# Hybrid attention trunk on one core: the softmax division moved from the score tiles to the output of the product with the values

## The chip, the cores and the metric

The kernel runs on one core of one Trainium2 chip. Its time is the device time of one execution, in microseconds (us). A core has five engines that work side by side, each through its own queue in order: TensorE (PE: matmuls and transposes, with PEld for its weight loads), VectorE (DVE), ScalarE (ACT), GpSimd (POOL) and SyncE (SP, which issues the DMAs). They wait for one another through semaphores. SBUF is the working memory of 128 partitions, PSUM the memory into which PE writes its results, used by this kernel in banks of 128x512 numbers.

## The reference

The model is a trunk of two layers over 1024 latent tokens and 256 context tokens of width 1024, with 16 heads of 64. Layer 0 is a two-dimensional neighbourhood attention with a learned bias, layer 1 a sliding window attention (128 to either side) with 4 groups of keys and values for the 16 heads and one sink logit per head. In both, each latent token reads its neighbourhood and all context tokens in one softmax; in layer 0 the context tokens attend to one another as well. Each layer ends with a gated feed-forward network with a short convolution. What the change touches is the softmax and the product behind it:

```python
def attend(q, k, v, bias=None, mask=None, sink=None):
    s = jnp.einsum('...qngd,...knd->...ngqk', q, k).astype(jnp.float32) * (HEAD_DIM ** -0.5)
    if bias is not None:
        s = s + bias.astype(jnp.float32)
    if mask is not None:
        s = jnp.where(mask, s, NEG_INF)
    if sink is not None:
        sink_col = ...
        s = jnp.concatenate([s, sink_col], axis=-1)
    p = jax.nn.softmax(s, axis=-1)
    if sink is not None:
        p = p[..., :-1]
    return jnp.einsum('...ngqk,...knd->...qngd', p.astype(v.dtype), v)
...
    for i in range(DEPTH):
        ...
        h = modulate(rmsnorm(x, g_attn[i]), sh1, sc1)
        ...
        x = x + gt1 * (o @ w_out)
        if not last:
            o_c = attend(q_c, k_c, v_c, sink=sink).reshape(bsz, n_ctx, D_MODEL)
            ctx = ctx + gt1c * (o_c @ w_out)
        h = modulate(rmsnorm(x, g_ffn[i]), sh2, sc2)
        x = x + gt2 * conv_ffn(h, ffn_w_up[i], ffn_conv_w[i], ffn_conv_b[i], ffn_w_down[i])
        ...
```

## The kernel before

**Precision.** Matmuls run on numbers of type fp32r. An operand is split into a high part (its copy in fp32r) and a low part (the difference to the original), and a product is made of two or three matmuls: names that end in hi and lo, such as whi, wlo, pthi, ptlo, are these parts. A projection of one tile of 128 tokens is 8 x 3 matmuls (mm<-whi,h0hi and its two partners).

**Stages.** The program runs the modulation and the norms, then the attention of layer 0 (about 60 to 720 us of the profile), its output projection and feed-forward network, the attention of layer 1 (about 1720 to 2190 us) and again projection and network. The change touches the two attention stages only.

**Units.** `plan_su` plans one unit of attention. A unit has two halves k = 0 and 1, each a block of 128 queries of one head. In layer 0 (`plan_na_su`) a unit is a head pair hp (of 8), a slice su (of 5: four of 256 latent queries, and one, su = 4, of the 256 context queries) and a head e of the pair; its halves are the two blocks of the slice. That makes 80 units. In layer 1 (`plan_sw_su`) a unit is a group g (of 4), a block j of 128 queries (of 8) and a pair of heads pr; its halves are the two heads. That makes 64 units. For each half:

1. PE makes the scores, in layer 0 in PSUM banks named s, in layer 1 in one wide tile with a place for each half. Queries lie on the partitions, keys along the row.
2. DVE passes over the scores (bias or mask added, sign turned, the row's extreme found) and writes them to the tile S in SBUF.
3. ACT takes the exponential in place and adds up each row: the sum goes to the small tile sm.
4. DVE takes the reciprocal of sm (one instruction per half in layer 0, one for both halves in layer 1).
5. DVE or ACT multiplies the whole of S by it, 256 to 640 columns: `TENSOR_SCALAR S<-S,sm` or `ACTIVATE S<-S,sm`.

Then, for both halves together and in two or three groups of up to two key blocks:

6. PE transposes the blocks of S (pt<-idr,S) into a PSUM bank pt, so that keys lie on the partitions.
7. ACT writes the high part (pthi<-pt), DVE the low part (ptlo<-pt,pthi).
8. PE multiplies both by the values (pv<-pthi,v and pv<-ptlo,v), all into one bank pv. Values are split too, with high and low part side by side, so that the first 64 partitions of pv hold the product with the high part and the other 64 that with the low part.
9. ACT copies one half of pv to SBUF (pvup<-pv), and DVE adds the two into the output tile osb (osb<-pv,pvup), where the outputs lie transposed: head dimension on the partitions, two heads one above the other, queries along the row.

An output tile osb covers 256 queries in layer 0 (both heads e) and 512 in layer 1 (four blocks j); when full it is stored by a DMA on SP's queue (o_dram<-osb), or, in the last head pair or group, split at once for the output projection.

**What sets the order.** `Sched` gets every operation with its candidate engines, an assumed duration, what it reads and writes, a key, and the buffers that it takes (acq) and gives back (rel). It then plays the whole stage through, on each engine always the ready operation with the lowest key, and an operation may only start if its buffers are free: for pt two PSUM banks, for pv one, for qsq, osb and the parts two SBUF buffers each. Where an operation has two candidate engines, the one that would finish it first by this reckoning gets it. The result is one fixed order per engine, in which the instructions are issued. So a change of one operation moves many others. Between the units stand, by their keys, the projections for the next head pair or group; they are most of what PE has to do besides the units, and there are fewer of them per unit in layer 1 than in layer 0.

All instructions come through a helper at line 79, so the profile's rows are told apart by their tile names.

Of the kernel before, what the change touches and what calls it, by code (L numbers as in the profile page):

```python
# [241 lines left out]
def trunk_kernel(ctx, tc, xperm, xseq, cc, wmod, bmod, gnorm, na_wqkv, na_gq, na_gk, na_bias, na_wo,  # L242
# [187 lines left out]
    def t_dve(n):  # L430
        return 0.065 + n / 960.0

    def t_act(n):
        return 0.094 + n / 1200.0
# [164 lines left out]
    def plan_su(sc, key, I, units, groups, psa, wk, reads, write, n_add, wide=None, at=None):  # L599
# [33 lines left out]
        if wide is not None:  # L633
            for k in range(2):
# [4 lines left out]
                def scores(e, k=k, nl=nl):  # L639
                    if k == 0:  # L640
                        J["sm"] = tiny.tile([P, 2, 2], F32, tag="sm", name="sm", bufs=4)
# [15 lines left out]
        for k in range(2):  # L657
# [3 lines left out]
            def ctx_part(e, k=k):  # L661
                u = J["u", k]
                if k == 0:
                    J["sm"] = tiny.tile([P, 2, 2], F32, tag="sm", name="sm", bufs=4)
# [29 lines left out]
        for k in range(2):  # L694
            n = TC + units[k]["nl"]
# [6 lines left out]
            if wide is None:  # L702
                sc.op("dve", 0.08, rec, reads=[K("P", k)], writes=[K("r", k)], key=key)
            elif k == 0:
                sc.op("dve", 0.09, rec, reads=[K("P", 0), K("P", 1)], writes=[K("r", 0), K("r", 1)], key=key)
# [446 lines left out]
    def plan_na_su(n):  # L1152
# [47 lines left out]
        ok = ("osb", hp, su)  # L1200

        def write(sc, J, K):
# [6 lines left out]
            if e == 0:  # L1209
                return  # L1210
            if hp < HP - 1:
# [11 lines left out]
        plan_su(sc, key, I, units, groups, psa, wk, reads, write, 1)  # L1223
# [1084 lines left out]
    def plan_sw_su(n):  # L2308
# [29 lines left out]
        ok = ("osb", g, j // 4, pr)  # L2338

        def write(sc, J, K):  # L2340
# [17 lines left out]
        plan_su(sc, key, I, units, [lst[i:i + 2] for i in range(0, len(lst), 2)], psa, wk, reads, write, 2, wide, at)  # L2358
# [169 lines left out]
```

## Time and profile before

| | |
|---|---|
| time, median of 3 runs (lowest to highest) | 2945.76 us (2944.11 to 2946.61) |
| span of the profiled execution, which is the time that the page gives of it | 2945.7 us |
| PE busy | 2826.0 us, 96% |
| PEld busy | 2459.7 us, 84% |
| DVE busy | 2383.5 us, 81% |
| ACT busy | 1725.9 us, 59% |
| POOL busy | 790.4 us, 27% |
| DMA | 367.51 MB, mean 125 GB/s |
| exponentials of score halves | 288 |
| transposes of score blocks | 1280 |

In the rows of the profile, `out<-in` gives the tiles, then come the shapes as partitions x elements. In the timeline a row begins with its start and its length in us, and a bracket at its end gives the idle time of its engine before it and what ended that. In the tables of groups, `x76` is a count, and behind the first bar stand the busy time in us and the mean length in ns. In the list of waits the engine that waited stands left of the arrow, its releaser right of it, then the total in us, how often, and the longest. A table of stretches gives busy us per engine, the clock that PE was granted (1.00 is full), the share of the DMA engines and GB/s. The score pass in layer 1 appears as `CUSTOM_DVE_ANT_0 S<-wide,bandt,small` followed by a read of its accumulator m; in the program's order it is written `ISA`.

### The profile page before, as it was taken

To read this page: it belongs to the slowest core of one execution; us is meant where nothing else is said; L and a number is where in the kernel's file an instruction comes from. 1 tells how busy PE (TensorE), PEld (TensorE's weight loads), DVE (VectorE), ACT (ScalarE), POOL (GpSimd) and SP (SyncE) were. 2 spreads that over 40 slices of the span, in tenths; PEclk is the share of its full clock that TensorE was granted. 3 is DMA by queue.
4 is the path that set the end of the run, shared out by engine and by line. 5 is a ranking of instruction groups with operands and counts; after the bars stand their busy time and mean duration, and the time that the engine had idled before them with its cause. 6 is when DMAs were issued, how large, how long until landed. Compare 5 with 4: busy or idle time off the path is not lost. (4 is left out here: it accounts for less than half of the span.)

```text
span 2945.7 us, 45913 instructions
## 1 busy us (share of the span) xinstructions
PE 2826.0 (96%) x16344; PEld 2459.7 (84%) x16344; DVE 2383.5 (81%) x4788; ACT 1725.9 (59%) x3389; POOL 790.4 (27%) x867
## 2 busy tenths in 40 slices
PE   6999999999999999999989999999899999999999
PEld 4999999998889977777778888988877687777787
DVE  7888888889688777877886878888877887888757
ACT  4777777778456544444544568887763544444443
POOL 2222222122100033313430135544521123433200
PEclk9999999999999999999999999999999999999999
DMA  6222222215645544444464630100144333233655
GB/s 239 62 86 79 87 62 74 86 60 153 229 162 183 178 150 147 140 150 148 154 240 163 194 119 30 33 12 14 73 127 145 102 103 100 90 100 129 242 158 186
DMA packets 138838, 367.51 MB, mean 125 GB/s; under 512 B 20848, under 2 KB 30448, under 8 KB 137200
## 3 DMA queue, kind: packets, MB, share of 16 engines
q1 hardware_dynamic: 138608, 364.57, 37.5%
q8 instruction: 129, 2.11, 0.3%
q14 instruction: 101, 0.83, 0.1%
HBM read 297.53 MB, written 66.98 MB: 124 GB/s over the span
## 5 line engine op out<-in xcount | busy, mean ns | idle before, releaser
L79 DVE TENSOR_TENSOR wlo<-wraw,whi 128x512 fp32r<-128x512 f32 (+1 forms) x245 | 298.4, 1218 | 40.4 <-ACT whi L79 38.3
L79 ACT ACTIVATE whi<-wraw 128x512 fp32r<-128x512 f32 (+1 forms) x264 | 212.3, 804 | 173.0 <-PE ud L79 45.4
L79 ACT ACTIVATE whi<-s 128x1024 fp32r<-128x1024 f32 (+1 forms) x120 | 113.2, 944 | 256.6 <-PE uc L79 222.6
L79 DVE TENSOR_TENSOR ptlo<-pt,pthi 128x512 fp32r<-128x512 f32 (+2 forms) x384 | 221.3, 595 | 51.6 <-ACT pthi L79 49.3
L79 DVE SCALAR_TENSOR_TENSOR u<-c,cv,u 128x1023 f32<-128x1023 f32 x176 | 252.2, 1448 | 8.9 <-ACT u L79 7.4
L79 PE MATMUL dn<-glo,whi 128*128 128x512 f32 x616 | 241.9, 393 | 5.8 <-DVE glo L79 5.7
L79 PE MATMUL dn<-ghi,whi 128*128 128x512 f32 x616 | 241.8, 393 | 4.2 <-ACT ghi L79 4.2
L79 ACT ACTIVATE S<-S,m 128x640 f32<-128x640 f32 (+3 forms) x288 | 220.9, 768 | 41.6 <-DVE m L79 28.6
L79 PE MATMUL dn<-ghi,wlo 128*128 128x512 f32 x616 | 241.3, 392 | 0.0
L79 ACT ACTIVATE pthi<-pt 128x512 fp32r<-128x512 f32 (+2 forms) x384 | 193.6, 524 | 72.8 <-PE pt L79 62.7
L79 PE MATMUL pt<-idr,S 128*128 128x128 f32 x1280 | 195.3, 276 | 2.6 <-DVE ptlo L79 1.0
L79 ACT ACTIVATE ghi<-graw 128x512 fp32r<-128x512 f32 x154 | 95.7, 627 | 153.7 <-PE dn L79 93.0
L79 PE MATMUL mm<-whi,h0hi 128*128 128x384 f32 x512 | 181.6, 355 | 1.6 <-ACT qraw L79 1.6
L79 POOL TENSOR_TENSOR u<-u 128x1024 f32<-128x1024 f32 x42 | 107.5, 2561 | 270.3 <-issue 105.7
L79 PE MATMUL mm<-wlo,h0hi 128*128 128x384 f32 x512 | 172.0, 336 | 0.0
L79 DVE TENSOR_TENSOR glo<-graw,ghi 128x512 fp32r<-128x512 f32 x145 | 106.0, 735 | 79.3 <-ACT ghi L79 78.8
L79 POOL TENSOR_TENSOR qy<-qv,mhalf 128x4 f32<-128x4 f32 (+2 forms) x120 | 125.6, 1047 | 164.2 <-DVE qv L79 156.7
L79 PEld LDWEIGHTS pt<-idr,S 128*128 128x128 f32 x1280 | 150.3, 142 | 12.0 <-DVE ptlo L79 1.9
L79 PE MATMUL pv<-ptlo,v 128*128 128x256 f32 (+1 forms) x688 | 151.4, 294 | 6.9 <-DVE ptlo L79 6.5
L79 DVE TENSOR_TENSOR wlo<-s,whi 128x1024 fp32r<-128x1024 f32 (+1 forms) x114 | 132.9, 1166 | 29.2 <-ACT whi L79 28.3
L79 PE MATMUL ua<-t12hi,whi 128*128 128x512 f32 x352 | 141.3, 401 | 12.3 <-ACT c L79 8.5
L79 PE MATMUL pv<-pthi,v 128*128 128x256 f32 (+1 forms) x688 | 146.6, 285 | 4.1 <-DVE osb L79 2.0
(344 smaller groups left out, 9180.3 us busy)
## 6 DMA issues: line engine op xcount, KB each, us to landing
wraw<-in_w_up_dram SPq DMA_DIRECT2D x132, 512.0 KB, 3.4
wm<-in_wmod_dram SPq DMA_DIRECT2D x80, 512.0 KB, 4.2
wraw<-in_w_down_dram SPq DMA_DIRECT2D x44, 512.0 KB, 3.6
graw<-g_dram SPq DMA_DIRECT2D x44, 512.0 KB, 4.5
wraw<-in_w_down_dram SPq DMA_DIRECT2D x88, 256.0 KB, 3.0
graw<-g_dram SPq DMA_DIRECT2D x66, 256.0 KB, 2.8
slab<-in_na_wqkv_dram SPq DMA_DIRECT2D x32, 384.0 KB, 3.2
woraw<-in_na_wo_dram SPq DMA_DIRECT2D x24, 512.0 KB, 4.8
```

The source lines that it names most:

```text
L79: r = f(*a, **k)
```

## The change

The scalings of S (step 5) and the reciprocals ahead of them (step 4) are gone: S stays undivided through transposition, split and the product with the values. A new object `Late` stands for one pair of units: in layer 0 the two heads e of a slice, in layer 1 the blocks j and j + 1 of one pair of heads. Its small tile t holds the four row sums that the exponentials of the two units write. When the second unit has its output added, `Late.plan` plans four more operations:

1. `rec`: one reciprocal of all four sums (DVE, 128x4).
2. `wide_`: a copy that spreads the four factors over 64 columns each, to a tile rb of 128x256 (ACT or DVE; rb takes one of the two buffers of qsq).
3. `tr`: two transposes of rb on PE into one of the two pt banks, which puts the factor of each query and head where the output's elements lie.
4. `mul`: DVE multiplies the output tile's 256 columns by that bank, which is then free.

Only then is the output tile stored or split. The sums are ready after the last exponential of the pair, so the first three can run before the product with the values is done; the fourth needs the added output. In all there are 40 such chains in layer 0 and 32 in layer 1, and 288 scalings and 224 reciprocals fewer. Since the order of each engine is made anew, other instructions move as well.

```diff
+    class Late:
+        def __init__(self, I, n):
+            self.I, self.n, self.t = I, n, None
+        def part(self, *a):
+            return _Half(self, *a)
+        def plan(self, sc, key, psa, wk, nsq, out, reads, writes):
+            I, n = self.I, self.n
+            toks = [I + ("sum", a, b) for a in range(n) for b in range(2)]
+            def rec(e):
+                dve.reciprocal(self.t[:, 1, :, :], self.t[:, 0, :, :])
+            sc.op("dve", 0.09, rec, reads=toks, writes=[I + ("r",)], key=key)
+            def wide_(e):
+                self.rb = wk.tile([P, nsq], F32, tag="qsq", name="rb", bufs=2)
+                copy(e, self.rb[:, :n * P].rearrange("p (a d) -> p a d", d=DH),
+                     self.t[:, 1, :, :].rearrange("p a b -> p (a b)").unsqueeze(2).to_broadcast([P, 2 * n, DH]))
+            sc.op(("act", "dve"), (t_act(n * P), t_dve(n * P)), wide_, reads=[I + ("r",)], writes=[I + ("rb",)], key=key,
+                  acq=[("qsq", I + ("rb",), 1)])
+            def tr(e):
+                self.pt = psa("pt", F32)
+                for a in range(n):
+                    pe.transpose(self.pt[:, a * P:(a + 1) * P], self.rb[:, a * P:(a + 1) * P], idf)
+            sc.op("pe", 0.107 * n, tr, reads=[I + ("rb",)], writes=[I + ("rt",)], key=key, acq=[("pt", I + ("rt",), 1)],
+                  rel=[I + ("rb",)])
+            def mul(e):
+                dve.tensor_tensor(out=out(), in0=out(), in1=self.pt[:, :n * P], op=ALU.mult)
+            sc.op("dve", t_dve(n * P), mul, reads=[I + ("rt",)] + reads, writes=writes, key=key, rel=[I + ("rt",)])
...
             def exp(e, k=k, nl=nl, ne=n + sink):
                 s = J["S", k]
                 act.activation(s[:, :ne], s[:, :ne], AF.Exp, bias=J["m", k][:, (1 if nl else 0):(2 if nl else 1)],
-                               scale=-1.0, accum_out=J["sm"][:, k, 0:1])
-            sc.op("act", t_act(n) + 0.187, exp, reads=parts, writes=[K("P", k)], key=key)
-            def rec(e, k=k):
-                if wide is None:
-                    dve.reciprocal(J["sm"][:, k, 1:2], J["sm"][:, k, 0:1])
-                else:
-                    dve.reciprocal(J["sm"][:, :, 1], J["sm"][:, :, 0])
...
-            def scale(e, k=k, n=n):
-                s = J["S", k][:, :n]
-                if e == "act":
-                    act.activation(s, s, AF.Copy, scale=J["sm"][:, k, 1:2])
-                else:
-                    ENG[e].tensor_scalar(out=s, in0=s, scalar1=J["sm"][:, k, 1:2], scalar2=None, op0=ALU.mult)
-            sc.op(("dve", "act"), (0.063 + 0.6 * n / 960.0, t_act(n)), scale, reads=[K("r", k)], writes=[K("P", k)], key=key)
+                               scale=-1.0, accum_out=norm.sum(k))
+            sc.op("act", t_act(n) + 0.187, exp, reads=parts, writes=[K("P", k), norm.tok(k)], key=key)
...
+            f["late", su].plan(sc, key, psa, wk, 256, lambda: f["o", su], [], [ok])
...
+            if j % 2:
+                lt.plan(sc, key, psa, wk, 320, lambda: f["o", pr][:, (j % 4 - 1) * P:(j % 4 + 1) * P], [], [ok])
```

More of the change, by code (lines that the diff above doesn't have):

```diff
@@ new lines, in trunk_kernel, with __init__, sum, tok @@
+    class _Half:
+        def __init__(self, late, *ab):
+            self.late, self.ab = late, ab
+        def sum(self, k):
+            L = self.late
+            if L.t is None:
+                L.t = tiny.tile([P, 2, L.n, 2], F32, tag="sm", name="sm", bufs=4)
+            a, b = [k if x is None else x for x in self.ab]
+            return L.t[:, 0, a, b:b + 1]
+        def tok(self, k):
+            a, b = [k if x is None else x for x in self.ab]
+            return self.late.I + ("sum", a, b)
@@ L600, in plan_su @@
+    def plan_su(sc, key, I, units, groups, psa, wk, reads, write, norm, wide=None, at=None):
         J = {}
@@ L1200, in plan_na_su @@
         ok = ("osb", hp, su)
+        if e == 0:
+            f["late", su] = Late(("late0", hp, su), 2)
         def write(sc, J, K):
@@ L1221, in write @@
                               key, [ok], [ok])
-        plan_su(sc, key, I, units, groups, psa, wk, reads, write, 1)
+        plan_su(sc, key, I, units, groups, psa, wk, reads, write, f["late", su].part(None, e))
     for k in range(KT):
@@ L2338, in plan_sw_su @@
         ok = ("osb", g, j // 4, pr)
+        if j % 2 == 0:
+            f["late", pr] = Late(("late1", g, j // 2, pr), 2)
+        lt = f["late", pr]
         def write(sc, J, K):
@@ L2356, in write @@
                 op1.split(j // 4, (j // 4, kt), 512, lambda: O[j // 4, pr], lambda a: a[:, kt, :], key, [ok], [ok])
-        plan_su(sc, key, I, units, [lst[i:i + 2] for i in range(0, len(lst), 2)], psa, wk, reads, write, 2, wide, at)
+        plan_su(sc, key, I, units, [lst[i:i + 2] for i in range(0, len(lst), 2)], psa, wk, reads, write, lt.part(j % 2, None), wide, at)
     for j in range(0, KT, 2):
```

11 lines of the change are left out of this document (removed).

## The prediction

> **What bounds the kernel now.** I read the page's first part, then the table of stretches, then the waits of TensorE (PE) in the two attention stretches, and last the timeline around the longest of them. The page's head says that PE is the engine to watch:
>
> ```profile
> span 2945.7 us, 45913 instructions
> PE 2826.0 (96%) x16344; PEld 2459.7 (84%) x16344; DVE 2383.5 (81%) x4788; ACT 1725.9 (59%) x3389; POOL 790.4 (27%) x867
> ```
>
> The span of this execution, 2945.7 us, is the median of the shown runs (2945.76 us) to a tenth, so I add and subtract from 2945.7. The table of stretches (length, then busy us of PE, PEld, DVE, ACT and POOL, then the granted clock) separates the two layers. Layer 0's attention lies in 60 to 690 us, layer 1's in 1720 to 2190 us:
>
> ```profile
> 60.00:690.00 630.00, 625.27 (x4481) 595.56 (x4479) 528.68 (x1881) 462.64 (x1198) 141.48 (x189) 1.00 0.26 76
> 1720.00:2190.00 470.00, 435.79 (x2949) 407.72 (x2949) 398.56 (x1070) 370.55 (x895) 227.34 (x446) 0.97 0.13 42
> ```
>
> In layer 0 PE is idle for 630 - 625.27 = 4.7 us and its clock is full: that stretch is PE's own work. In layer 1 PE is idle for 470 - 435.79 = 34.2 us, and a granted clock of 0.97 takes away up to 0.03 x 470 = 14.1 us more. So layer 1 has at most 48.3 us to give back, and layer 0 next to nothing. The waits of PE in layer 1 (us in total, times, longest) name the engine:
>
> ```profile
> PE wide L79 <- DVE m L79: 16.4, 26, 1.8
> PE pv L79 <- DVE ptlo L79: 6.2, 7, 1.7
> PE pt L79 <- DVE ptlo L79: 1.3, 3, 0.7
> ```
>
> DVE is 398.56 / 470 = 85% busy there, and PE waits for its score pass (which frees the wide score bank) and for the low half of the transposed scores. Two places show what stands ahead of such a wait. In the first it is an instruction that the change removes:
>
> ```profile
> 2150.86 2.77 POOL L79 TENSOR_TENSOR o0lo<-oraw,o0hi 128x512 fp32r<-128x512 f32 x2 [2.34 <-ACT o0hi L79]
> 2151.01 2.97 DVE L79 TENSOR_SCALAR S<-S,sm 128x640 f32<-128x640 f32 x2
> 2153.89 0.41 DVE L79 TENSOR_TENSOR ptlo<-pt,pthi 128x256 fp32r<-128x256 f32 x1
> 2154.36 0.39 PE L79 MATMUL pv<-ptlo,v 128*128 128x256 f32 x1 [1.74 <-DVE ptlo L79]
> ```
>
> Two scalings of score tiles take 2.97 us while POOL works beside them; the low half stands behind them, and PE is idle for 1.74 us. The usual length of one (min, median and max of the 76 on DVE in layer 1, ns) is 549:
>
> ```profile
> L79 DVE TENSOR_SCALAR S<-S,sm x76: 475/549/2201, 1765.5 to 2175.7; 128x640 f32<-128x640 f32 x63, 128x512 f32<-128x512 f32 x13
> ```
>
> In the second, no instruction of the change stands ahead:
>
> ```profile
> 2013.77 1.90 DVE L79 TENSOR_TENSOR v<-qraw,v 128x64 fp32r<-128x64 f32 x1
> 2015.60 0.87 DVE L79 CUSTOM_DVE_ANT_0 S<-wide,bandt,small 128x640 f32<-128x640 f32 x1
> 2017.33 0.58 PE L79 MATMUL wide<-kkc,q 128*128 128x256 f32 x1 [1.81 <-DVE m L79]
> ```
>
> **The change, part by part.** Removed are the scalings of the score tiles with their reciprocals. For the whole span, and then for the two stretches (DVE, ACT, clock):
>
> ```profile
> 0.00:2945.70 2945.70, 152.62 (x440) 54.33 (x72) 0.98 0.38 125
> 60.00:690.00 630.00, 87.60 (x279) 11.29 (x17) 1.00 0.26 76
> 1720.00:2190.00 470.00, 57.70 (x140) 40.56 (x52) 0.97 0.13 42
> ```
>
> Added are 72 chains: 8 head pairs x 5 slices = 40 in layer 0, and 4 groups x 4 pairs of blocks x 2 = 32 in layer 1. Each has one reciprocal (DVE), one copy of 128x256 that spreads the factors (by the program's order 21 on DVE and 19 on ACT in layer 0, 15 and 17 in layer 1), two PE transposes, and one DVE multiplication of 128x256 that reads PSUM. Their prices come from these rows, the PE rows being start and length:
>
> ```profile
> 304.45 0.38 PE L79 MATMUL pt<-idr,S 128*128 128x128 f32 x2
> 304.59 0.42 PE L79 MATMUL mm<-whi,h0hi 128*128 128x384 f32 x1
> 304.85 0.33 PE L79 MATMUL mm<-whi,h0lo 128*128 128x384 f32 x1
> 305.01 0.34 PE L79 MATMUL mm<-wlo,h0hi 128*128 128x384 f32 x1
> ```
>
> and for the other engines (busy us and mean ns of one behind the first bar):
>
> ```profile
> L79 DVE RECIPROCAL sm<-sm 128x2 f32<-128x2 f32 x64 | 10.1, 158 | 3.8 <-ACT S L79 3.4
> L79 DVE TENSOR_TENSOR modsb<-modsb,pt 128x256 f32<-128x256 f32 x28 | 11.7, 418 | 0.4
> L79 DVE TENSOR_SCALAR S<-S,sm 128x256 f32<-128x256 f32 x25 | 8.7, 351 | 0.4
> L79 ACT ACTIVATE st<-qn 128x256 fp32r<-128x256 f32 x80 | 33.1, 413 | 19.8 <-DVE qn L79 18.4 <-DVE sm L79 0.5
> ```
>
> PE: from the start of a pair of such transposes to the start of the second matmul behind it is 304.85 - 304.45 = 0.40 us; a matmul of 384 columns alone takes 0.17 from start to start, so a pair costs 0.23 us. That is 40 x 0.23 = 9.2 us in layer 0 and 32 x 0.23 = 7.4 us in layer 1, together 16.6 us on the busiest engine.
>
> Layer 0: PE's work is continuous, so the 9.2 us go on the path. Its 4.7 us of idle time could hide a part, which makes the ends 4.5 and 9.2; I take 9.2, since the pairs are put between matmuls that were waiting for nothing. The fences below show PE in layer 0, fourth head pair, slice 3, second head: pt<-idr,S is the transposition of scores, pt<-idr,rb that of the factors, mm is the projection for the next head pair. Before:
>
> ```order
> L79 MATMUL pv<-ptlo,v 128x256 x2
> L79 MATMUL pv<-pthi,v 128x256 x2
> L79 MATMUL pv<-ptlo,v 128x256 x2
> L79 MATMUL pt<-idr,S 128x128
> L79 MATMUL mm<-whi,h0hi 128x384
> L79 MATMUL mm<-whi,n1lo 128x384
> L79 MATMUL mm<-wlo,h0hi 128x384
> L79 MATMUL pt<-wm,cpad 32x256 x4
> L79 MATMUL pv<-pthi,v 128x128
> ```
>
> PE at the same slice in the changed program:
>
> ```order
> L79 MATMUL pv<-ptlo,v 128x256 x2
> L79 MATMUL pv<-pthi,v 128x256 x2
> L79 MATMUL pv<-ptlo,v 128x256 x2
> L79 MATMUL pt<-idr,S 128x128
> L79 MATMUL mm<-whi,h0hi_119 128x384
> L79 MATMUL mm<-whi,h0lo_123 128x384
> L79 MATMUL mm<-wlo,h0hi_119 128x384
> L79 MATMUL pt<-idr,rb 128x128 x2
> L79 MATMUL pv<-pthi,v 128x128
> ```
>
> The pair has come in ahead of the last product with the values, behind matmuls that need nothing of it; nothing idle was there to take it. The relief of DVE and ACT in layer 0 I cost at nothing, since PE hides them; without that cover they would be worth little more than the 4.7 us.
>
> Layer 1: DVE loses 57.7 us and gains 32 x 0.158 + 32 x 0.418 + 15 copies at 0.35 to 0.42 (351 and 418 ns as bounds, the middle taken) = 5.1 + 13.4 + 5.8 = 24.3 us, so 33.4 us less: 365 of 470, or 78% in place of 85%. ACT loses 40.56 and gains 17 x 0.413 = 7.0, so 33.6 less: 72% in place of 79%. What PE gets of it I can only bound. The low end is the waits that end on the low half, 6.2 + 1.3 = 7.5 us, and the same share of the clock (7.5 / 34.2 x 14.1 = 3.1): 10.6 us. The high end is all 48.3. DVE's order in layer 1 speaks for the inner part. ISA S is the score pass, ISA m its second half, which yields the row's extreme. Before, at the 79th pass of 128:
>
> ```order
> L79 TENSOR_TENSOR ptlo<-pt,pthi 128x512
> L79 RECIPROCAL sm<-sm 128x2
> L79 TENSOR_SCALAR S<-S,sm 128x640
> L79 TENSOR_TENSOR ptlo<-pt,pthi 128x256
> L79 TENSOR_SCALAR S<-S,sm 128x640
> L79 TENSOR_TENSOR osb<-pv,pvup 64x128 x2
> L79 TENSOR_TENSOR ptlo<-pt,pthi 128x512 x2
> L79 ISA S,m_24103<-wide,bandt,small 128x640
> L79 ISA m_24103 128x1
> ```
>
> DVE at the same pass after the change:
>
> ```order
> L79 TENSOR_TENSOR ptlo<-pt,pthi 128x512 x2
> L79 ISA S,m_23923<-wide,bandt,small 128x640
> L79 ISA m_23923 128x1
> L79 TENSOR_TENSOR ptlo<-pt,pthi 128x256
> L79 TENSOR_REDUCE qv<-qsq 128x5
> L79 TENSOR_TENSOR v<-qraw,v 128x64
> L79 TENSOR_SCALAR qv<-qv 128x5
> L79 ISA S,m_23952<-wide,bandt,small 128x640
> L79 ISA m_23952 128x1
> ```
>
> Low halves and score passes, the two things that PE waits for, now follow one another without scalings between. Against that stands the second place above, where PE's wait was for score passes alone and the change has nothing to take away. I take 25 us, a little over half of 48.3 and a little under the middle of the ends (29.4). Layer 1 then comes out at 7.4 - 25 = -17.6 us.
>
> A rule that bears on the size: the scaling at 2151.01 and POOL's subtraction ran over the same time, and the scaling took 2.7 times as long as two of the median. The Trainium skill, SBUF — State Buffer, section Who interferes with whom, says that a VectorE instruction in a two-port mode, `tensor_scalar` and copies among them, and GpSimd shut each other out for the whole instruction; the trace agrees here (2.97 us beside POOL's 2.77). By that rule the 76 scalings on DVE in layer 1 become at most 15 copies that can collide, and if nothing but such collisions were recovered the sum would be that of the second rival below. The sum does not use it.
>
> Waits that the chain adds: the reciprocal on DVE waits for ACT's exponential, as the two old ones did, with low halves queued behind it; the transposes wait for the copy, and stand several rows behind it in PE's order; the multiplication waits for the transposes and for the addition just ahead of it on its own engine. The output tile leaves for DRAM after the multiplication, some 0.4 us later, on SP's queue; behind it are loads of weights and of bias (the latter planned 8 units ahead of their use), and the tile is read back only by the output projection at the stretch's end. I cost that at nothing: the time up to there covers it, except for the last head pair and the last group, whose tail gets 0.4 + 0.2 us longer at its end and loses a reciprocal and a scaling (0.16 + 0.55) at its front. No DMA is moved past another in a way that the path sees.
>
> Sum: 2945.7 + 9.2 + 7.4 - 25 = 2937.3 us.
>
> **Rivals.** First, all of layer 1's loss comes back, as layer 0 (DVE 84% busy, PE idle for 4.7 us) shows to be possible: 2945.7 + 16.6 - 48.3 = 2914. Against it: POOL is busy for 227 of 470 us there, not 141 of 630, and fewer projection matmuls stand by as filling.
>
> Second, only the waits behind removed work go, and the back and forth between PE's score product and DVE's score pass stays: 2945.7 + 16.6 - 10.6 = 2951.7, slower by 0.2%. For it: 16.4 of the 34.2 us are waits of that kind. It decides as soon as fewer than 10.7 us come back.
>
> Third, slower through one bank: the transposed factors hold one of the two pt banks until the multiplication, and the score transposes behind must share the other. A wait of PE for such a bank costs now 0.4 us (1.3 over 3 times) to 0.7. If each of the 32 holds in layer 1 costs one of 0.6, that is 19 us: 2956. It turns the forecast into a loss from 25 - 16.6 + 5.9 = 14.3 us of new waits, 0.45 us for each hold. Against it: the hold is short where the transposes stand late, as in the order shown.
>
> Fourth, the added transposes count as idle time for the clock: 7.4 us more on 34.2 would take the clock's loss from 14.1 to 17.1, and the sum to 2940.3. Against it: layer 0 had the clock at 1.00 with all its transposes. The Trainium skill, TensorE: Matmul & The Clock Gate, section on PE-mode transpose, says that a transpose does not count as busy for the gate; the trace of layer 0 does not bear that out as a loss.
>
> **Chances.** A difference under 0.2% (5.9 us) is about what a measurement of this kernel cannot tell from none. The forecast's case, 22.5 to 40 us recovered, 2922 to 2939.8: 0.40. More than that, towards the first rival: 0.07. Between 10.7 and 22.5 recovered, within 0.2% of before, the fourth rival among it: 0.27. Slower: 0.26, half the second rival, half the third. So 0.47 faster, 0.27 the same, 0.26 slower. The range leaves 0.07 below 2922 and 0.13 above 2958, beyond the third rival's 2956; the likeliest case's own range is 2922 to 2940.
>
> **What would show it.** In the new profile: PE's busy time in layer 0 some 9 us longer with idle time still near 5 us; layer 1 some 18 us shorter, PE's waits for DVE's score pass and low half well under 16.4 and 7.5, the clock above 0.97. The prediction is wrong if layer 0 doesn't grow (then the pairs were hidden), if layer 1's idle time stays near 34 us (second rival), or if PE waits for a pt bank in front of score transposes (third).

## The result, and the profile after

The changed kernel takes 2957.12 us (median of 5 runs, 2949.28 to 2960.03) where the kernel before takes 2944.84 (5 runs, 2942.73 to 2946.61): a ratio of 1.0039, with a 95% interval of 1.0025 to 1.0053. It is slower by 0.4%, or some 11 us. The forecast was 2937.3, faster by 0.3%; the stated range, 2922 to 2958, holds the time, but on its slower end.

The profiled execution of the changed kernel is the fastest of the five, 2949.28 us with a span of 2947.1. So its profile shows only 1.4 us of the 11 (its span against the 2945.7 of before's), and the size of each cause is taken from the runs below, not from this one profile. The page's head after:

```profile
span 2947.1 us, 45970 instructions
PE 2829.2 (96%) x16488; PEld 2466.0 (84%) x16488; DVE 2323.1 (79%) x4535; ACT 1690.0 (57%) x3351; POOL 771.2 (26%) x862
```

DVE lost 60 us of work (2383.5 to 2323.1) and ACT 36, and PE, which has 144 transposes more, gained 3. The table of stretches after, in the same two stretches as in the prediction:

```profile
60.00:690.00 630.00, 626.94 (x4524) 601.20 (x4523) 493.23 (x1704) 450.04 (x1184) 126.08 (x167) 1.00 0.24 74
1720.00:2190.00 470.00, 437.05 (x3047) 409.87 (x3046) 376.24 (x994) 346.34 (x866) 229.54 (x465) 0.99 0.14 48
```

In layer 1 DVE went from 398.56 to 376.24 us (80% of the stretch, 78% forecast) and ACT from 370.55 to 346.34 (74%, 72% forecast). PE's idle time went from 34.2 us to 470 - 437.05 = 33.0: it stayed. The waits of PE in that stretch after:

```profile
PE wide L79 <- DVE m L79: 15.5, 25, 2.4
PE pv L79 <- DVE ptlo L79: 7.2, 6, 3.1
PE pt L79 <- DVE ptlo L79: 1.5, 3, 0.7
PE pt L79 <- DVE osb L79: 1.4, 3, 1.0
```

The first three were 16.4, 6.2 and 1.3; the fourth is new. The waits that the change was expected to shorten are all there, and the longest ones are longer (3.1 us for the low half and 2.4 for the score pass, 1.7 and 1.8 before). The groups of the new instructions (min, median and max in ns) cost about what the prediction had for them:

```profile
L79 PE MATMUL pt<-idr,rb x144: 270/272/421, 90.7 to 2193.2; 128*128 128x128 f32 x144
L79 DVE COPY rb<-sm x36: 277/294/915, 89.8 to 2186.8; 128x256 f32<-128x256 f32 x36
L79 ACT ACTIVATE rb<-sm x36: 402/414/423, 161.9 to 2180.2; 128x256 f32<-128x256 f32 x36
```

### The profile page after: what moved, and what is told of

It reads as the page before. It is cut to its first block, busy times and chain, and to the rows that moved or that the text cites. A ratio compares the mean times of both kernels' runs of the same rounds, so it can differ in the third digit from the quotient of the medians.

```text
span 2947.1 us, 45970 instructions
## 1 busy us (share of the span) xinstructions
PE 2829.2 (96%) x16488; PEld 2466.0 (84%) x16488; DVE 2323.1 (79%) x4535; ACT 1690.0 (57%) x3351; POOL 771.2 (26%) x862
## 5 line engine op out<-in xcount | busy, mean ns | idle before, releaser
L79 PEld LDWEIGHTS pt<-idr,S 128*128 128x128 f32 x1280 | 149.5, 141 | 14.9 <-DVE ptlo L79 2.3
```

Source lines behind the costliest of these rows:

```text
L79: r = f(*a, **k)
```

## The experiments

A kernel's runs are compared with the runs of the kernel before on the same chip. Where us are given for a ratio, they are the ratio's distance from 1 times 2945. Three things are to be kept apart: the **relief** (reciprocals and scalings of the score tiles gone), the **new order** (the planner's new sequence for everything else), and the **chain** (reciprocal, copy, transposes and multiplication on the output).

### Relief, order and chain apart

The first kernel has the order of the kernel before, with reciprocals and scalings planned but issuing nothing. The whole division is left out of what it computes.

```diff
             def rec(e, k=k):
-                if wide is None:
-                    dve.reciprocal(J["sm"][:, k, 1:2], J["sm"][:, k, 0:1])
-                else:
-                    dve.reciprocal(J["sm"][:, :, 1], J["sm"][:, :, 0])
+                return
...
             def scale(e, k=k, n=n):
-                s = J["S", k][:, :n]
...
+                return
```

> The order of the kernel before, with the scalings of the score tiles and their reciprocals left out (so the outputs stay undivided) and nothing put in their place. It prices the relief of DVE and ACT alone. Theory A (PE's own work sets the time; its waits in layer 1 hang on bursts on DVE and not on DVE's load): 2939 to 2943 us, 2 to 6 under before, PE's waits for the score pass in layer 1 still 12 us or more. Theory B (the forecast's relief is real and is lost elsewhere): about 2920 us, 25 under before, those waits under 8 us.

Measured: 2917.67 us, ratio 0.9911 [0.9896, 0.9927], or -26 us. The time is that of theory B; PE's waits for the score pass in layer 1 stay at 14.9 us, as theory A had it. The second kernel is the changed one with the four functions of the chain returning at once; it too leaves out the whole division, and issues the same instructions as the first in the new order.

```diff
             def rec(e):
-                dve.reciprocal(self.t[:, 1, :, :], self.t[:, 0, :, :])
+                return
...
             def mul(e):
-                dve.tensor_tensor(out=out(), in0=out(), in1=self.pt[:, :n * P], op=ALU.mult)
+                return
```

> The order of the changed kernel, with the four instructions of each chain (reciprocal, spreading copy, two transposes, multiplication) left out, so the outputs stay undivided. It issues the same instructions as the first run of this call, in the new order. Theory A: within 4 us of that run, so about 2941 us, 16 under the changed kernel. Theory C (the new order is the loss, whatever it carries): 2948 us or more, 8 or more above that run.

Measured: 2930.66 us, ratio 0.9957 [0.9942, 0.9971], or -13 us. So the relief is worth 26 us; the new order alone takes half of it back (2930.66 - 2917.67 = 13.0 us); and the chain takes the rest and 11 us more. The changed kernel again, beside the runs below:

> The changed kernel once more, beside the runs below and the kernel before. The two layers' instructions and orders are those of the two one-layer kernels put together, which stood at +4.6 us (layer 0) and -4.1 us (layer 1). If the layers simply add, 2945 us; if the first measurement (2957 us, five executions) holds, 2955 to 2959 us and something joins the two.

Measured: 2955.74 us, ratio 1.0039 [1.0027, 1.0051]. The chain costs 1.0039 - 0.9957 = 0.0082, or 24 us. To split it, the transposes alone were left out; the multiplication then takes the output tile by itself, so that the division is again left out:

```diff
             def tr(e):
-                self.pt = psa("pt", F32)
-                for a in range(n):
-                    pe.transpose(self.pt[:, a * P:(a + 1) * P], self.rb[:, a * P:(a + 1) * P], idf)
+                return
...
-                dve.tensor_tensor(out=out(), in0=out(), in1=self.pt[:, :n * P], op=ALU.mult)
+                dve.tensor_tensor(out=out(), in0=out(), in1=out(), op=ALU.mult)
```

> The changed kernel, its order kept, without the 144 transposes of the factors; the output tile is multiplied by itself instead of by the factors. Everything else of the chain stays. Theory D (the chain costs because of PE's own work): 16.6 us, less at most 4, under the changed kernel of this call, near the 2931 us of the same order without any chain, plus 2 to 5. Theory E (the chain costs through DVE and ACT, of whose relief it takes a third back): 8 us or less under the changed kernel.

Measured: 2940.31 us, ratio 0.9988 [0.9976, 1.0000]. The 144 transposes cost 2955.74 - 2940.31 = 15.4 us, where 16.6 was forecast, and reciprocals, copies and multiplications the other 9, each with an uncertainty of some 5 us. The transposes alone on the kernel before, as pairs whose result nobody reads, so that the planner may put them wherever PE has room:

```diff
+    def plan_pair(sc, key, I, psa):
+        def tr(e):
+            pt = psa("pt", F32)
+            for a in range(2):
+                pe.transpose(pt[:, a * P:(a + 1) * P], idf, idf)
+        sc.op("pe", 0.214, tr, reads=[], writes=[I], key=key, acq=[("pt", I, 1)], rel=[I])
...
+            plan_pair(sc, key, ("pair0", hp, su), psa)
...
+            if j % 2:
+                plan_pair(sc, key, ("pair1", g, j, pr), psa)
```

> The kernel before, planned anew with 72 pairs of unused transposes, one at the end of each pair of units, their bank free at once; scalings stay. Theory D: 40 x 0.23 = 9.2 us in layer 0 and 7.4 us in layer 1, together +16.6: 2961 us, and no less than 2956. If idle time of PE in layer 1 takes its share: +9, 2954 us.

Measured: 2946.98 us, ratio 1.0005 [0.9996, 1.0014], or +1.5 us: a tenth of what the same instructions cost in the chain. That is a net figure, and it does not show that they cost PE nothing. The table of stretches of this kernel, with marks that mean the same work in each kernel: from the start to the first matmul of layer 0's network on the latents (ua), and from the first projection of layer 1 to the first such matmul there:

```profile
0.00:1034.40 1034.40, 992.49 (x7109) 936.63 (x7109) 837.81 (x2413) 686.62 (x1568) 196.22 (x236) 0.99 0.38 123
1719.49:2260.04 540.55, 510.38 (x3377) 466.51 (x3376) 448.04 (x1137) 397.61 (x933) 247.80 (x465) 1.00 0.18 62
```

Beside the rows of the kernel before (the next ones below), the first stretch, which holds 40 of the 72 pairs, is 6.0 us longer and PE is busy 7.3 us more in it; the second is 9.5 us shorter, at a granted clock of 1.00 instead of 0.97. All executions show a higher clock: 0.9889 in the mean of 11, against 0.9864 in 29 of the kernel before, and 0.0025 of 2945 us is up to 7.4 us. In the chain the clock goes the other way: 0.9858 with the transposes (5 executions), 0.9880 without them (12). As an estimate without the clock I take each execution's time multiplied by its mean granted clock, as if PE set the pace throughout. By it the transposes cost 8.9 us on the kernel before (give or take 1.8) and 8.9 us in the chain (give or take 4.8). These pairs also differ from the chain's in that they wait for no copy and hold no bank for a multiplication, and they change the order of the rest; the estimate is too coarse to give any of these a share.

Where the time lies is seen in the stretches between these marks. Before:

```profile
0.00:1028.35 1028.35, 985.16 (x7028) 927.77 (x7029) 841.26 (x2435) 684.82 (x1560) 183.41 (x222) 0.99 0.38 124
1711.61:2261.64 550.03, 513.74 (x3314) 473.08 (x3312) 454.45 (x1142) 403.04 (x941) 241.73 (x454) 0.97 0.18 61
```

With the relief alone:

```profile
0.00:1026.25 1026.25, 983.18 (x7029) 929.15 (x7030) 776.87 (x2135) 670.73 (x1540) 182.13 (x222) 0.99 0.38 124
1708.27:2238.94 530.67, 501.66 (x3314) 467.64 (x3312) 411.14 (x1001) 367.68 (x889) 234.53 (x454) 0.98 0.19 63
```

With relief and new order:

```profile
0.00:1029.79 1029.79, 987.30 (x7028) 932.25 (x7029) 787.10 (x2159) 670.75 (x1538) 165.38 (x200) 0.99 0.38 124
1712.03:2249.28 537.25, 505.82 (x3314) 466.85 (x3312) 407.80 (x985) 370.07 (x889) 239.90 (x471) 0.98 0.19 63
```

And the changed kernel:

```profile
0.00:1036.77 1036.77, 993.33 (x7108) 938.32 (x7109) 808.57 (x2260) 676.67 (x1557) 164.73 (x200) 0.99 0.38 123
1721.94:2264.76 542.82, 509.23 (x3377) 469.71 (x3376) 426.12 (x1063) 375.23 (x906) 240.07 (x471) 0.99 0.18 62
```

Read down the first rows: PE is idle for 43.2, 43.1, 42.5 and 43.4 us up to the mark, all alike, while its busy time goes 985, 983, 987, 993. Between the second and third of these PE runs the same matmuls, and yet is busy 4 us longer. That is mostly the clock: added up from the clock records of the traces (the length of each times one minus its clock), 10.2, 10.2, 13.7 and 10.2 us are lost in these four rows. Between the first and the last, at an equal loss, PE is busy 8.2 us longer; the relief is worth 2 us here. Other profiles agree: in seven kernels with layer 0 as before the mark comes at 1028.35 to 1031.41 us, in five with layer 0 changed at 1036.77 to 1039.59, and in the changed kernel without its transposes at 1030.90. The third row shows one more thing that the order did: with the same program of instructions, 22 instructions went from GpSimd (POOL, 222 to 200) to DVE, which is busy 10 us longer; PE is idle no longer for it.

### Layer by layer

Each of the three was measured in each layer. The relief in layer 0 alone and in layer 1 alone, in the order of before (the division of that layer is left out):

```diff
             def rec(e, k=k):
+                if wide is None:
+                    return
...
             def scale(e, k=k, n=n):
+                if wide is None:
+                    return
```

with `wide is not None` for layer 1.

> Kernel before, with the reciprocals and scalings left out in layer 0 only and every other instruction where it was; outputs of layer 0 stay undivided. One of two halves of the relief that was worth -27 us when both layers left them out. The forecast's step (relief in layer 0 worth nothing, PE hides DVE and ACT there): 2942 to 2946 us. If the relief of layer 0 is worth what its DVE and ACT time suggests (88 and 11 us taken off), well below that: 2930 to 2938.

> Kernel before, with the reciprocals and scalings left out in layer 1 only. The forecast's step (25 us of PE's waits and of the clock come back): 2917 to 2924. The second rival (only the waits behind the removed work go, 10.6 us): 2933 to 2936. If relief is additive over the layers, this and the run for layer 0 sum to -27 against before.

Measured: layer 0 2938.6 us, 0.9963 [0.9950, 0.9975], -10.9 us; layer 1 2925.61 us, 0.9921 [0.9907, 0.9934], -23.3 us. Then the order of a change made in one layer only, with that layer's chain left out, and with it that layer's division:

> The changed order in layer 0 only, with the chain's instructions (reciprocal, copy, transposes, multiplication) left out there; layer 1 as before. Same instructions as the run with the relief of layer 0 alone, in another order. If the new order costs in layer 0 (TensorE has no slack there): 3 to 8 us above that run, and the chain of layer 0 then costs what is left up to the layer-0-only change's 2949 us. If the order costs only in layer 1: level with it within 2 us.

> The changed order in layer 1 only, with the chain's instructions left out there; layer 0 as before. Same instructions as the run with the relief of layer 1 alone. If the new order's 13 us lie in layer 1: 8 to 13 us above that run, and the chain of layer 1 (32 pairs, copies, multiplications) costs the rest up to the layer-1-only change's 2940.5 us, which is 7.4 us by the forecast's price of the pairs. If the order is free here: level within 2 us, and then the chain costs 15 us or more in layer 1.

Measured: 2943.39 us, 0.9983 [0.9973, 0.9993], for layer 0; 2931.94 us, 0.9943 [0.9930, 0.9955], for layer 1. Of what the relief in layer 0 is worth little lies in layer 0: of the 8.9 us by which that kernel's profile is shorter than before's (2936.8 for 2945.7), 2.9 lie up to the mark (1025.48 for 1028.35), and its layer 1, whose instructions are as before, takes 545.61 us at a clock of 0.98 (550.03 at 0.97). The order takes back 0.0020 (5.9 us) in layer 0 and 0.0022 (6.5 us) in layer 1. Last the change itself in one layer, complete; the other layer keeps its scalings. For layer 0 only, in layer 1:

```diff
-            if j % 2:
-                lt.plan(sc, key, psa, wk, 320, lambda: f["o", pr][:, (j % 4 - 1) * P:(j % 4 + 1) * P], [], [ok])
...
-        plan_su(sc, key, I, units, [lst[i:i + 2] for i in range(0, len(lst), 2)], psa, wk, reads, write, lt.part(j % 2, None), wide, at)
+        plan_su(sc, key, I, units, [lst[i:i + 2] for i in range(0, len(lst), 2)], psa, wk, reads, write, None, wide, at)
```

where plan_su plans the old reciprocals and scalings if it is given None.

> The change in layer 0 alone; layer 1 as before. Theory A: 40 pairs of transposes at 0.23 us, 9.2 us, less at most 2 us: 2952 to 2955 us. Theory C or a contended bank in layer 0: 2958 us or more. If the pairs were hidden there: 2945 us.

> The change in layer 1 alone; layer 0 as before. Theory A: 7.4 us of transposes, less 2 to 6 us of relief: 2946 to 2951 us. Theory B, the forecast's term for layer 1 (-17.6 us): 2927 us.

Measured: layer 0 only 2949.19 us, 1.0016 [1.0007, 1.0026]; layer 1 only 2940.48 us, 0.9990 [0.9979, 1.0000]. Since 4.7 - 2.9 is not 11, the two were run once more with the whole change on one chip:

> The change in layer 0 only. If the gap lies in the calls, this or the layer-1 part stands higher against before than in the first call (+4.6 us): +8 to +10 by the pairs' full price. If it is real, +4 to +5 again.

> The change in layer 1 only. If the gap lies in the calls: -1 to +2 us against before. If it is real: -4 to -5 us again.

> The changed kernel, on the same chip and in the same call as the changes in one layer alone. If 10 us are lost only where both layers are changed: 2954 to 2958, some 10 us above the sum of the two parts. If the gap was a difference between chips and calls: within 4 us of the sum of the two parts, whatever that is here.

Measured: layer 0 only 2951.55 us, 1.0014 [1.0004, 1.0023]; layer 1 only 2943.13 us, 0.9986 [0.9977, 0.9995]; the whole change 2956.8 us, 1.0036 [1.0022, 1.0050]. So +4.1 and -4.1 us, and +10.6 together: the gap is no matter of chips. In us, with the two measurements of a part's change averaged:

| | relief | new order | chain | the change |
|---|---|---|---|---|
| layer 0 alone | -10.9 | +5.9 | +9.4 | +4.4 |
| layer 1 alone | -23.3 | +6.5 | +13.3 | -3.5 |
| sum of the two | -34.2 | +12.4 | +22.7 | +0.9 |
| both together | -26.2 | +13.5 | +23.9 | +11.2 |

Order and chain add up over the layers; the relief does not. By these ratios 8 of the 10 us lie there, though each relief has an uncertainty of 3 to 5 us, so that this place is likely rather than shown.

An estimate puts most of the gap down to the clock. The mean granted clock is 0.9861 to 0.9864 in the executions of the kernel before that stand beside these, 0.9872 and 0.9868 with layer 0 alone changed, 0.9871 twice with layer 1 alone, and 0.9858 to 0.9866 with both. By the estimate without the clock (time multiplied by granted clock) the change costs 7.3 us in layer 0 alone (8.2 and 6.5), gains 0.9 in layer 1 alone (0.4 and 1.3) and costs 9.0 with both (8.3 and 9.7): of the gap 2.6 us are left, with an uncertainty of about 3. The reliefs come to -6.1 and -18.2 us, and to -22.3 together, so they nearly add up. The stretch of layer 1 in the layer-0-only kernel, whose layer 1 is that of before:

```profile
1724.23:2265.69 541.46, 504.00 (x3313) 462.74 (x3312) 453.07 (x1141) 402.14 (x941) 240.91 (x454) 0.99 0.18 62
```

It is 8.6 us shorter than before's 550.03 with nothing changed in it; PE is busy 9.7 us less at a granted clock of 0.99 instead of 0.97, and idle for 37.5 us as against 36.3. (In a second profile of this kernel it was 546.33 us at 0.98.) What changes before layer 1 thus moves how much of layer 1 runs at a lower clock. The traces show what the clock follows. Its records run in periods of 3.41 us. In the twenty traces of this case, from 60 us on, all 166 periods at full clock in which PE was idle for more than 1.9 us were followed by one at half clock; of the 16330 others 70 were. In the stretch of layer 1 the clock falls seven times before and three times in the layer-0-only kernel, with the same instructions and nearly the same idle time. I take it that waits which fall into one period lower the clock and the same waits spread over two do not, so that any shift ahead of them matters; this wasn't tried by itself. Why both changes together end at the lower clock stays open.

### The price of the pairs, and of the places

The layer-1-only change with rb and its transposes in fp32r:

```diff
-                self.rb = wk.tile([P, nsq], F32, tag="qsq", name="rb", bufs=2)
+                self.rb = wk.tile([P, nsq], F32R, tag="qsq", name="rb", bufs=2)
...
-                self.pt = psa("pt", F32)
+                self.pt = psa("pt", F32R)
```

> The change in layer 1 alone, with the factors' tile and its transposes in fp32r, the type of the other transposes of this kernel (59 to 87 ns from start to start where the fp32 ones take 109), so the factors are rounded to that type. Theory D: 32 pairs cheaper by 0.05 to 0.1 us each, 1.6 to 3.2 us under the kernel with the change in layer 1 alone: about 2938 us. Theory E: as that kernel, 2940.5 us.

Measured: 2940.57 us, 0.9987 [0.9978, 0.9995], level with the layer-1-only change. The median length of a transpose fell from 272 to 225 ns. The 1.6 to 3.2 us that theory D expected of it lie within the two intervals, so this run doesn't settle whether the pairs are paid by their length. The layer-1-only change with the old scalings kept in the plan as operations that issue nothing:

```diff
+        if norm is not None:
+            for k in range(2):
+                n = TC + units[k]["nl"]
...
+                sc.op(("dve", "act"), (0.063 + 0.6 * n / 960.0, t_act(n)), lambda e: None, reads=[K("r", k)], writes=[K("P", k)], key=key)
```

> The change in layer 1 only, but the two scalings and the reciprocal of each unit stay in the planner's reckoning with their old durations and issue no instruction, so that the rest is planned as if they were still there; the chain is planned besides. If the new order's 6 us in layer 1 come from what the planner puts into the place of the scalings: some 6 us below the layer-1-only change, 2933 to 2936. If they come from the chain's own places: level with it within 2 us, 2938 to 2943. If the reserved places cost instead: above it.

Measured: 2944.68 us, 0.9994 [0.9985, 1.0003]; the layer-1-only change on the same chip stood at 0.9986. Keeping the places won nothing, so the 6 us of the order are not the price of the missing scalings in the planner's reckoning. The kept places pushed 30 instructions over to GpSimd. Layer 1 with the places kept:

```profile
1713.77:2259.55 545.78, 514.34 (x3378) 476.20 (x3376) 420.32 (x1032) 375.04 (x908) 256.69 (x501) 0.97 0.18 62
```

and without:

```profile
1711.67:2255.47 543.80, 510.66 (x3378) 471.19 (x3377) 426.88 (x1064) 376.07 (x906) 240.64 (x471) 0.99 0.18 62
```

PE is idle for 31.4 and 33.1 us in them, but the clock differs (0.97 and 0.99), so the comparison isn't one of the places alone. A part of the order's price shows in PE's waits in layer 1, from the first projection to the last product with the values. With the new order there and no chain they are:

```profile
PE wide L79 <- DVE m L79: 18.3, 27, 2.4
PE pv L79 <- DVE ptlo L79: 5.3, 5, 3.1
```

With the relief alone, in the old order, they are 14.9 and 2.7 us (rows below). What else the price consists of is left open.

### What took the place of the scalings

Even with the relief of layer 1 alone, and none of the chain, PE waits for the score pass as before. Its waits there, in the stretch from the first projection to the last product with the values:

```profile
PE wide L79 <- DVE m L79: 14.9, 23, 1.8
PE pv L79 <- DVE ptlo L79: 2.7, 4, 1.6
```

The waits for the low half fall (6.2 to 2.7 us), those for the score pass stay (16.4 and 14.9). In the changed kernel PE's longest wait in layer 1 is the one below; it is at the same place of the program and 3.05 us long in its two other profiles as well (timeline: start, length, engine):

```profile
1898.31 3.59 POOL L79 TENSOR_TENSOR wlo<-slab,whi 128x768 fp32r<-128x768 f32 x2
1898.40 1.75 DVE L79 SCALAR_TENSOR_TENSOR qt<-qt,qv 128x5 f32<-128x5 f32 x1
...
1900.19 1.72 DVE L79 SCALAR_TENSOR_TENSOR qy<-qt,qy 128x5 f32<-128x5 f32 x1
1901.84 0.68 DVE L79 TENSOR_TENSOR ptlo<-pt,pthi 128x512 fp32r<-128x512 f32 x1
...
1902.57 0.79 PE L79 MATMUL pv<-ptlo,v 128*128 128x256 f32 x2 [3.07 <-DVE ptlo L79]
```

Two instructions of DVE on 128x5 numbers take 1.75 and 1.72 us, each beside one of two subtractions of a weight slab on GpSimd, and the low half stands behind them. The layer-1-only change, and the kernel before, with that subtraction made in four pieces:

```diff
+            if e == "pool":
+                for c in range(0, 768, 192):
+                    pool.tensor_tensor(out=lo[:, c:c + 192], in0=self.raw[i][:, c:c + 192], in1=hi[:, c:c + 192].bitcast(F32),
+                                       op=ALU.subtract)
+                return
```

> The change in layer 1 only, and GpSimd's subtraction of a weight slab (128x768, 1.8 us) made in four pieces of 192 columns. If VectorE is held for the length of the GpSimd instruction beside it, the longest waits of PE in layer 1 (3.1, 2.4 and 2.1 us) fall to about 1 us and some 4 to 8 us come back: 2934 to 2939. If the hold is a matter of total GpSimd time or the waits have another cause: level with the layer-1-only change, 2940 to 2945.

> The kernel before with the same four pieces and nothing of the change. If such holds bound layer 1 before the change as well (the scaling of 2.97 us beside GpSimd): 2937 to 2942. If they took the place of the scalings only after the change: level with before within 2 us. Extra instructions on GpSimd, 3 for each slab, could also cost a little: up to 2 us more than before.

Measured: layer 1 changed with pieces 2938.82 us, 0.9977 [0.9968, 0.9986], or -6.8 us; before with pieces 2944.57 us, 1.0000 [0.9991, 1.0009]. The small instructions of layer 1, undivided subtraction (layer-1-only change):

```profile
L79 DVE TENSOR_TENSOR qt<-qy x40: 134/160/1791, 1721.1 to 2127.8; 128x5 f32<-128x5 f32 x32, 128x1 f32<-128x1 f32 x8
L79 DVE SCALAR_TENSOR_TENSOR qt<-qt,qv x40: 133/164/1820, 1721.3 to 2129.9; 128x5 f32<-128x5 f32 x32, 128x1 f32<-128x1 f32 x8
L79 DVE SCALAR_TENSOR_TENSOR qy<-qt,qy x40: 135/166/1724, 1721.5 to 2130.4; 128x5 f32<-128x5 f32 x32, 128x1 f32<-128x1 f32 x8
```

and in four pieces:

```profile
L79 DVE TENSOR_TENSOR qt<-qy x40: 131/160/795, 1720.4 to 2125.3; 128x5 f32<-128x5 f32 x32, 128x1 f32<-128x1 f32 x8
L79 DVE SCALAR_TENSOR_TENSOR qt<-qt,qv x40: 128/164/598, 1720.6 to 2127.5; 128x5 f32<-128x5 f32 x32, 128x1 f32<-128x1 f32 x8
L79 DVE SCALAR_TENSOR_TENSOR qy<-qt,qy x40: 134/165/585, 1720.8 to 2127.9; 128x5 f32<-128x5 f32 x32, 128x1 f32<-128x1 f32 x8
```

The longest falls from 1820 to 795 ns. The one of 795 stands beside another subtraction (o0lo, 1.27 us); beside the slab's the longest is now 598 ns, and the median piece takes 600 ns on GpSimd where the whole takes 1.8 us. So they were held for up to the length of the instruction beside them. Such holds aren't new: before, two of these instructions stood beside the slab's subtraction for 1.70 and 1.78 us, and in the changed kernel four for 1.72 to 1.80. PE's waits with pieces:

```profile
PE wide L79 <- DVE m L79: 15.5, 26, 2.4
PE pv L79 <- DVE ptlo L79: 4.0, 7, 0.9
```

In the layer-1-only change they are 16.0 and 7.3 us, the longest 2.4 and 3.1. So the longest wait for a low half falls from 3.1 to 0.9 us, and all of them from 7.3 to 4.0. The time gained over the layer-1-only change, 0.0009 or 2.7 us, is of the same size but within the two intervals. The waits for the score pass stay, in this kernel (15.5) and in every other (14.9 to 18.6 us): these holds do not cause them. With 0.9977 this is the fastest of the complete kernels, ahead of both the kernel before and the changed one.

## Why the prediction was wrong

**What bounds the kernel.** That layer 1 has something to give and that relief is worth some 25 us there was right: -23.3 us measured. That layer 0 is "PE's own work" holds within its stretch, where the relief brought 2 us and left PE's idle time as it was. What was wrong is to price a change of layer 0 in layer 0 alone: the relief there, costed at nothing, made the whole run 10.9 us shorter, most of it in stages whose instructions are as before. Nor were the 14.1 us of clock in layer 1 a fixed loss of that layer: it came out at 0.97, 0.98 and 0.99 with the same instructions.

**The step that failed** is the term "I take 25 us", which was to be what PE gets net of the new load on DVE and ACT, with the new order at no price. By the table layer 1 gets 23.3 - 6.5 of the order, and of the chain's 13.3 us there only 7.4 were in the sum as pairs, which leaves 5.9 for copies, reciprocals and multiplications: 23.3 - 6.5 - 5.9 = 10.9 us instead of 25. (The 5.9 is uncertain by some 4 us; in the profiles the chain makes the stretch of layer 1 7.2 us longer, 536.56 to 543.80, which is hardly more than the pairs.) The sum had no term for the order at all, though the fences of the prediction showed how much it moved. In both layers together the order costs 13 us, as much as half the relief.

**Layer 0**: the +9.2 us are borne out in place. Up to the mark the changed kernel takes 8.4 us more, PE is busy 8.2 us more (993.33 for 985.16) with its idle time unchanged, as the prediction's sign said, and without the transposes it is there 5.9 us earlier. But the whole run with layer 0 alone changed is only 4.4 us longer, because layer 1 behind it ran at a higher clock (0.98 and 0.99 in its two profiles, 0.97 before), which no term had. The price of the pairs, 16.6 us in all, came out at 15.4 in the chain and at 1.5 on the kernel before, and by the estimate without the clock at 8.9 in both: they do cost PE time, about half of the forecast, and the rest of either figure goes with the clock.

**Both layers together**: the sum of the parts as measured, about +1 us, is still no loss. The 10 us that come on top were in no term and no rival; by the estimate without the clock all but 2.6 of them go with the clock. From the forecast's 2937.3 us it is thus +14.1 for layer 1 (-3.5 for -17.6), -4.8 for layer 0 and +10.3 for what the two do together.

**The rivals.** The first (all of layer 1's loss back, 2914) fails. The second (10.6 us come back, 2951.7) had the size that layer 1 gave, and its core holds: PE's waits for the score pass, 16.4 us before, are 15.5 after and 14.9 with the scalings simply gone. Its other half does not: the waits behind the removed work did not go but found new causes, 7.2 us for the low half as against 6.2. The third (a pt bank held, 2956) came nearest in time by chance and isn't borne out by the waits: those of PE for a bank that the multiplication frees (pt behind osb) come to 1.4 us, not 19, and those behind the low half to 1.5 as against 1.3. The fourth (transposes lower the clock) is not settled: 144 transposes added to the kernel before raised the mean granted clock (0.9864 to 0.9889), and those of the chain went with a lower one (0.9880 without them, 0.9858 with them). In layer 1, where its loss was to be, the changed kernel's clock was 0.99 for 0.97.

**The rule that was weighed.** The collision of a scaling with GpSimd was taken up for instructions in a two-port mode alone. The Trainium skill, SBUF — State Buffer, section Who interferes with whom, also says that a VectorE instruction with two inputs in SBUF contends with a GpSimd instruction that reads SBUF. The traces agree: the qt and qy rows above, of two inputs and normally 0.16 us, stood for up to 1.82 us beside such a subtraction. So the collisions did not go with the scalings: small instructions, held for 1.7 us and more beside that neighbour twice before, were so held four times.

## What to carry to other kernels

Where a planner makes the order, give the new order a term of its own in the sum, of either sign, and bound it: here it cost half of what the removed work was worth. Leave the suspected work out in place and measure, since a removal that keeps the order separates relief from rearrangement. A difference between two whole runs doesn't price the stage that was changed: it also holds what the change did to the granted clock of the stages behind. So put the stretch between two marks, with its clock, beside the total. When a wait ends on an instruction that stands behind a long one, ask which other instruction will stand there when that one is gone, and whether the neighbour that stretched it is still running.

## What was not expected of the hardware

- The same instructions of layer 1 took 550.03, 546.33 and 541.46 us in three profiles (one of the kernel before, two of the layer-0-only kernel), at granted clocks of 0.97, 0.98 and 0.99, with a nearly equal idle time of PE in the first and the last. A profile's stage times are not finer than that in this program.
- The granted clock moved in periods of 3.41 us. All 166 periods at full clock in which PE was idle for more than 1.9 us were followed by one at half clock, and 70 of 16330 others (twenty traces, from 60 us on).
- 144 fp32 transposes of 128x128, 270 ns long each, cost 1.5 us [-1.2, +4.1] added to the kernel before, at a mean clock of 0.9889 for 0.9864, and 15.4 us in the chain, at 0.9858 for 0.9880 without them.
- A VectorE instruction on 128x5 numbers takes 0.16 us, and up to 1.8 us beside a GpSimd subtraction of 768 columns; beside four subtractions of 192 columns it took up to 0.6 us.
